# Output projection by column halves, branch products in pairs, one merge gate held, in a two-layer hybrid encoder

## The chip, the core and the metric

The program runs on one core of a Trainium2 chip. Its engines are TensorE (PE, with its weight loads PEld), VectorE (DVE), ScalarE (ACT), GpSimd (POOL) and SyncE (SP, which issues the transfers). The metric is the device time of one execution in microseconds. Before the change it is 1779.11 us, the median of three runs (1778.2 to 1780.48).

## The reference, cut to what matters

Two layers run one after the other on x (512 tokens, 1024 channels, float32):

```python
p = split(x @ w_in + b_in)
y_a, y_b, y_c = three token mixers, each times its SiLU gate      # 512 channels each
branch = einsum('nbsc,ncd->nbsd', stack([y_a, y_b, y_c]), w_branch)
gates  = sigmoid(p['merge'].reshape(B, S, 3, D))
merged = sum_n gates[n] * branch[n]
out    = merged @ w_out
x      = LayerNorm(alpha * x + out) * ln_g + ln_b
```

The third mixer is an attention of four heads over 512 tokens. Head h fills channels 128h to 128h+127 of y_c, so that the last head's channels are the last quarter of the contraction of the third branch.

## The kernel before, in words

A float32 product is made of three products of rounded parts (hi by hi, lo by hi, hi by lo). Every weight chunk of 128 x 1024 is loaded by SP, rounded on ACT (`hi`, L274) and subtracted on POOL (`lo`, L275); for the first weights of a layer the subtraction is on DVE. Chunks take turns in two raw buffers and three hi and three lo buffers. Matrix products write one of four PSUM banks `mm`. The order on each engine is set by a scheduler that simulates the program when it is built; on the chip it is fixed, and an engine waits at an instruction whose inputs are not there.

What matters here is the end of a layer. For each query tile of 128 tokens, a head of the third mixer makes scores (`msc`, five products), a softmax (DVE maximum L646, ACT exp L648, DVE reciprocal and scale L649 and L650), four transposes (`mtr`, L653), four copies by DVE and ACT in turn (L655), and the values' products (`mo`, L659). The eight merge gates of the third branch (`mg`, 24 products each, L1158) are independent of the heads and are put between these steps. After the last head, `yc3h` and `yc3l` (L663 to L666) are its gated output in hi and lo parts.

`merge_branch` (L1079) makes the branch products `br`, one bank of 128 output channels after the other; within a bank the 12 products go in the order of channel blocks (`late`, L298), so that the last head's come last. DVE multiplies by the gate, adds to `acc`, and the sum is split again (`mm`, L1161: hi on ACT, lo on DVE).

w_out is loaded as eight chunks (`wo`, L1176 to L1197): number n holds 256 input channels (n % 4) and 512 output channels (n // 4). Three chunks lie in buffers of the large pool, two in buffers of `acc`, three in the rotating weight buffers. Token tiles 0 and 1 are made first, both column halves, then their common norm (L1248), then tile 2 with its norm and tile 3 with its norm. `residual` (L1199) adds alpha*x and takes statistics on DVE; `norm` (L1204) makes the inverse root from twelve small DVE operations and applies it by two passes over 1024 columns. The last tile's first half goes over ACT (L1221) and POOL (L1222). In layer 0 the result is also transposed back for layer 1 (`xps`, L421, and the split `xl`, L425), whose first products `st` (L498) run over halves of the tokens.

Of the kernel before, what the change touches and what calls it, by code (L numbers as in the profile page):

```python
# [200 lines left out]
def tile_encoder(ctx: ExitStack, tc: tile.TileContext, x, xt, positions, blocks, wuq, wuh, par_in, brow, lbp,  # L201
# [92 lines left out]
    def mm3(ps, lhs, rhs, kt, late=False):  # L294

        steps = [(a, b, k) for a, b in PASSES for k in range(kt)]
        if late:
            steps.sort(key=lambda t: (t[2], t[1]))  # L298
        for n, (a, b, k) in enumerate(steps):
            newest["product"] = nc.tensor.matmul(ps, lhs(a, k), rhs(b, k), start=n == 0, stop=n == 3 * kt - 1)  # L300

# [157 lines left out]
    def layer(l, x_src, need_next):  # L459
# [173 lines left out]
        def mla_head(h, prep, kr, v, gate):  # L633
# [3 lines left out]
            for qt in range(NT):  # L637
# [14 lines left out]
                for kb in range(NT):  # L652
                    nc.tensor.transpose(tr[:, kb * 128:kb * 128 + 128], p[:, kb * 128:kb * 128 + 128], ident)  # L653
# [425 lines left out]
        def merge_branch(n, dp, y, gates):  # L1079
            ys = ([p[0] for p in y], [p[1] for p in y])  # L1080
            wb = w_chunk(l, ("br", n, dp), (4, 256), f"wb{n}{dp}_{l}")
            for j in range(2):
                dt_, g = 2 * dp + j, gates[j]
                ps = fm(ys, f"br{n}{dt_}_{l}", lambda a, k: wb[a][:, k, 128 * j:128 * j + 128], kt=4, late=True)
# [73 lines left out]
        gates = [merge_gate(2, dt_, held[dt_ // 4][:, dt_ % 4]) for dt_ in range(KT)]  # L1158
# [14 lines left out]
        for t, src in ((lng, ln_g), (lnb, ln_b)):  # L1173
            nc.sync.dma_start(t, bass.AP(src.tensor, src.offset + l * D, [[0, 128], [512, 2], [1, 512]]))
        wo = []
        for n in range(8):  # L1176
            name = f"wo{n}_{l}"
            if n < 3:
# [3 lines left out]
            elif n < 5:  # L1182
# [57 lines left out]
        for half in range(2):  # L1240
            banks = [mm_bank(f"wo{tt}{half}_{l}") for tt in range(2)]
            for kp in range(4):
                for tt in range(2):
                    product(banks[tt], tt, half, (kp,))
            for tt in range(2):
                for j in range(2):
                    residual(tt, 2 * half + j, banks[tt][:, 256 * j:256 * j + 256])
        norm((0, 1))  # L1248
        for tt in (2, 3):
            for half in range(2):  # L1250
                cuts = [slice(0, 256), slice(256, 512)] if tt == NT - 1 and half else [slice(0, 512)]
                for cols in cuts:
                    bank = mm_bank(f"wo{tt}{half}{cols.start}_{l}")[:, cols]
                    product(bank, tt, half, range(4), cols)
                    for j in range(cols.start // 256, cols.stop // 256):
                        residual(tt, 2 * half + j, bank[:, 256 * j - cols.start:256 * j - cols.start + 256])
# [34 lines left out]
```

## Time and profile before

| | |
|---|---|
| median of 3 runs | 1779.11 us (1778.2 to 1780.48) |
| the profiled execution | 1780.54 us, of which the trace spans 1778.8 us |
| PE busy | 1745.7 us (98%) |
| DVE, ACT, POOL busy | 1048.8, 731.7, 574.6 us |
| granted PE clock, mean | 0.995 |
| layer 0, w_out products | 839.4 to about 889.8 us, then the first products of layer 1 |
| layer 1, w_out products | 1720.3 to 1768.9 us, then DVE alone and the last transfers |

PE is busy nearly all the time, so the places where it is not, or runs at a lower clock, are read one by one. The 40-slice line of the clock shows full speed everywhere: the slices are 44 us wide, and a lower clock over a few microseconds is only seen in narrow stretches.

### The profile page before, as it was taken

The numbers are of one execution on the slowest core, as the hardware profiler recorded it, in microseconds if no ns is written. First come the engines' busy times: TensorE is split into PE (matmuls) and PEld (weight loads), VectorE is DVE, ScalarE is ACT, GpSimd is POOL, SyncE is SP. The second block draws the span as 40 slices with busy tenths as digits, with TensorE's granted clock in tenths as the row PEclk, the third lists the DMA queues.
The fourth block names the chain that finished last, engine by engine and source line by source line (L and its number), as shares of the span: only waits on it lengthen the run. The fifth ranks groups of instructions, "written<-read, shape, count | busy, mean of one in ns | idle before, by whom it ended". The sixth has DMA issues, their size and how long they took to land.

```text
span 1778.8 us, 26441 instructions
## 1 busy us (share of the span) xinstructions
PE 1745.7 (98%) x10616; PEld 1451.2 (82%) x10616; DVE 1048.8 (59%) x1886; ACT 731.7 (41%) x1273; POOL 574.6 (32%) x338
## 2 busy tenths in 40 slices
PE   9999999999999999999999999999999999999987
PEld 7778978988888888887788888888888888888876
DVE  8888777443232566656577778775333225656566
ACT  6445453242424354433254355442424244434330
POOL 0412244233333243333213122532434332333341
PEclk9999999999999999999999999999999999999999
DMA  5223222223323222422242222222323222324222
GB/s 193 83 66 102 75 73 85 79 65 95 84 72 91 62 79 74 144 81 70 95 137 89 85 78 73 88 82 74 78 66 106 72 84 46 98 74 149 76 71 71
DMA packets 77146, 154.15 MB, mean 87 GB/s; under 512 B 37728, under 2 KB 37856, under 8 KB 77024
## 3 DMA queue, kind: packets, MB, share of 16 engines
q1 hardware_dynamic: 77024, 152.47, 28.0%
q8 instruction: 83, 1.36, 0.3%
q14 instruction: 39, 0.32, 0.1%
HBM read 148.15 MB, written 4.29 MB: 86 GB/s over the span
## 4 chain that ended last, share of the span: by engine, by line
PE 61%; DVE 4%; ACT 2%; DMA 1%; issue 1%; POOL 1%; SPq 0%; DVEq 0%; ACTq 0%
PE mg L300 14%; PE dl L300 6%; PE br L300 5%; PE wo L1236 5%; PE hf L300 4%; PE dv L317 4%; PE cq L300 2%; PE hq L300 2%; PE mo L659 2%; PE ckv L300 1%; PE hgg L300 1%; PE hv L317 1%; PE do L1016 1%; PE st L498 1%; PE qn L300 1%; PE dg L300 1%
## 5 line engine op out<-in xcount | busy, mean ns | idle before, releaser
L772 DVE TENSOR_TENSOR kk<-kk,fr 128x512 f32<-128x512 f32 x96 | 93.4, 992 | 32.8 <-ACT kc L742 21.7
L693 POOL TENSOR_TENSOR qq<-hq,fr 128x1024 f32<-128x1024 f32 x16 | 42.5, 2655 | 199.3 <-DVE fr L686 179.5
L771 DVE TENSOR_TENSOR qq<-qq,fr 128x512 f32<-128x512 f32 x96 | 75.3, 797 | 17.0 <-POOL qq L693 15.2
L1076 DVE TENSOR_SCALAR mg<-mg 128x512 f32<-128x512 f32 x32 | 53.4, 1680 | 54.0 <-ACT mg L1075 53.9
L895 DVE CUSTOM_DVE_ANT_0 zb<-dsb,con 128x256 f32<-128x256 f32 x64 | 23.3, 421 | 46.4 <-PE dsb L948 46.3
L764 DVE COPY_PREDICATED ha<-mask,hs 64x256 f32<-64x256 uint8 (+1 forms) x80 | 40.4, 505 | 16.7 <-PE hs L754 15.5
L655 ACT COPY mpt<-mtr 128x128 f32<-128x128 f32 x64 | 17.1, 266 | 77.7 <-DVE mpt L655 77.7
L275 POOL TENSOR_TENSOR wb_1l<-wb_1r,wb_1h 128x1024 fp32r<-128x1024 f32 x12 | 29.4, 2449 | 58.9 <-ACT wb_1h L274 45.0
L275 POOL TENSOR_TENSOR wb_0l<-wb_0r,wb_0h 128x1024 fp32r<-128x1024 f32 x12 | 29.4, 2448 | 58.8 <-ACT wb_0h L274 44.9
L878 DVE TENSOR_SCALAR dl<-dl,par,con 128x512 f32<-128x512 f32 x24 | 25.8, 1076 | 38.0 <-PE dl L300 37.9
L754 PEld LDWEIGHTS hs<-qq,kc 128*64 128x64 f32 x1024 | 33.3, 137 | 17.6 <-issue 8.8
L732 POOL TENSOR_SCALAR_AFFINE_SELECT ha<-hc 128x256 f32<-128x256 f32 x32 | 12.8, 424 | 105.0 <-ACT hc L727 104.8
L754 PE MATMUL hs<-qq,kc 128*64 128x64 f32 x1024 | 38.2, 225 | 5.6 <-DVE qq L771 5.6
L996 ACT ACTIVATE za<-za,dst 128x256 f32<-128x256 f32 x64 | 30.0, 471 | 33.4 <-DVE dst L990 33.4
L655 DVE COPY mpt<-mtr 128x128 f32<-128x128 f32 x64 | 18.5, 289 | 39.6 <-PE mtr L653 31.6
L713 POOL TENSOR_TENSOR hk<-kk,f 128x256 f32<-128x256 f32 x32 | 23.8, 745 | 51.5 <-DVE fr L775 51.5
L789 ACT COPY hkt<-hkt 128x384 f32<-128x384 f32 x32 | 15.4, 480 | 60.3 <-PE hkt L787 59.9
L1076 DVE TENSOR_SCALAR mgc<-mgc 128x512 f32<-128x512 f32 x16 | 24.8, 1547 | 25.0 <-ACT mgc L1075 25.0
L742 ACT COPY kc<-kk 128x512 f32<-128x512 f32 x64 | 37.6, 621 | 4.2 <-DVE kk L772 4.1
L650 DVE TENSOR_SCALAR mp<-mp,mst 128x512 f32<-128x512 f32 x32 | 35.6, 1112 | 0.9
L1201 DVE SCALAR_TENSOR_TENSOR res<-res,wo 128x256 f32<-128x256 f32 x32 | 12.1, 416 | 38.1 <-PE wo L1236 38.0
L659 PE MATMUL mo<-mpt,mv 128*128 128x128 f32 (+1 forms) x192 | 33.5, 309 | 0.0
(1509 smaller groups left out, 5408.5 us busy)
## 6 DMA issues: line engine op xcount, KB each, us to landing
wb_0r<-in_blocks_dram SPq DMA_DIRECT2D x12, 512.0 KB, 3.6
wb_1r<-in_blocks_dram SPq DMA_DIRECT2D x12, 512.0 KB, 3.6
w_0r<-in_blocks_dram SPq DMA_DIRECT2D x9, 512.0 KB, 3.6
w_1r<-in_blocks_dram SPq DMA_DIRECT2D x8, 512.0 KB, 3.6
w_2r<-in_blocks_dram SPq DMA_DIRECT2D x8, 512.0 KB, 3.5
w_3r<-in_blocks_dram SPq DMA_DIRECT2D x8, 512.0 KB, 3.6
wo_0r<-in_blocks_dram SPq DMA_DIRECT2D x8, 512.0 KB, 3.5
wo_1r<-in_blocks_dram SPq DMA_DIRECT2D x8, 512.0 KB, 3.5
```

Source lines behind the costliest of these rows:

```text
L275: (eng or nc.gpsimd).tensor_tensor(lo, raw, hi.bitcast(F32), ALU.subtract)
L300: newest["product"] = nc.tensor.matmul(ps, lhs(a, k), rhs(b, k), start=n == 0, stop=n == 3 * kt - 1)
L317: nc.tensor.matmul(ps, xs[a][2 * j + k][:, toks], w[b][:, k], start=j == 0 and n == 0, stop=j == 3 and n == 5)
L659: nc.tensor.matmul(o[:, cols], v[:, kb, h * 128:h * 128 + 128], pts[kb][:, cols], start=qt == 1 and kb == 0, stop=qt == NT - 1 and kb == N ...
L693: nc.gpsimd.tensor_tensor(qq, bcast(q, [[0, 2], [1, S]]), fr, ALU.mult)
L742: made = A.copy(fap(kc, 0, [[2 * m, R // 2], [m, 2], [1, m]]), fap(kk, 0, [[2 * m, R // 2], [S + m, 2], [1, m]]))
L754: mat = nc.tensor.matmul(sc[rows, to], kc[:, at], rhs, start=True, stop=True)
L764: ready = [V.copy_predicated(fap(a[rows], cols.start, [[128, NT], [1, wd]]), bcast(mk, [[0, NT], [1, wd]]), fap(sc[rows], cols.start, [[12 ...
L771: V.tensor_tensor(fap(qq, 0, dims), fap(qq, 0, dims), qf, ALU.mult)
L772: V.tensor_tensor(fap(kk, 0, dims), fap(kk, 0, dims), kf, ALU.mult)
L1076: V.tensor_scalar(g, g, 0.5, 0.5, ALU.mult, ALU.add)
L1236: nc.tensor.matmul(ps, ms[a][2 * kp + k][:, tt * 128:tt * 128 + 128], wo[4 * half + kp][b][k][:, cols], start=(kp, a, b, k) == (0, 0, 0, 0 ...
```

## The change

1. `merge_branch` makes its two banks together: 9 products of each bank over the first three channel blocks, then 3 products of each over the last block.
2. The last of the eight merge gates of the third branch is held: its first product gets a dependence on the last head's last transpose.
3. w_out goes by column halves over all four token tiles. In the first half the four banks advance chunk by chunk; in the second half the tiles go one after the other, each followed by its own norm. The chunks' places are exchanged: 0, 4, 5 lie in the large pool, 6 and 7 in `acc`, 1 to 3 in the rotating buffers.

```diff
+            if n == 0 and "hold" in newest:
+                after(newest["product"], newest.pop("hold"))
...
-                    nc.tensor.transpose(tr[:, kb * 128:kb * 128 + 128], p[:, kb * 128:kb * 128 + 128], ident)
+                    newest["turned"] = nc.tensor.transpose(tr[:, kb * 128:kb * 128 + 128],
+                                                           p[:, kb * 128:kb * 128 + 128], ident)
...
-            for j in range(2):
+            banks = [mm_bank(f"br{n}{2 * dp + j}_{l}") for j in range(2)]
+            for ks in (range(3), range(3, 4)):
+                for j, ps in enumerate(banks):
+                    for k, a, b in [(k, a, b) for k in ks for a, b in ((0, 0), (1, 0), (0, 1))]:
+                        newest["product"] = nc.tensor.matmul(
+                            ps, wb[a][:, k, 128 * j:128 * j + 128], ys[b][k], start=(k, a, b) == (0, 0, 0),
+                            stop=(k, a, b) == (3, 0, 1))
+            for j, ps in enumerate(banks):
                 dt_, g = 2 * dp + j, gates[j]
-                ps = fm(ys, f"br{n}{dt_}_{l}", lambda a, k: wb[a][:, k, 128 * j:128 * j + 128], kt=4, late=True)
...
-        gates = [merge_gate(2, dt_, held[dt_ // 4][:, dt_ % 4]) for dt_ in range(KT)]
+        gates = []
+        for dt_ in range(KT):
+            if dt_ == KT - 1:
+                newest["hold"] = newest["turned"]
+            gates.append(merge_gate(2, dt_, held[dt_ // 4][:, dt_ % 4]))
...
-            if n < 3:
+            if n in (0, 4, 5):
...
-            elif n < 5:
+            elif n > 5:
...
-        for half in range(2):
-            banks = [mm_bank(f"wo{tt}{half}_{l}") for tt in range(2)]
-            for kp in range(4):
-                for tt in range(2):
-                    product(banks[tt], tt, half, (kp,))
-            for tt in range(2):
-                for j in range(2):
-                    residual(tt, 2 * half + j, banks[tt][:, 256 * j:256 * j + 256])
-        norm((0, 1))
-        for tt in (2, 3):
-            for half in range(2):
-                cuts = [slice(0, 256), slice(256, 512)] if tt == NT - 1 and half else [slice(0, 512)]
...
+        banks = [mm_bank(f"wo{tt}0_{l}") for tt in range(NT)]
+        for kp in range(4):
+            for tt, ps in enumerate(banks):
+                product(ps, tt, 0, (kp,))
+                if kp == 3:
+                    for j in range(2):
+                        residual(tt, j, ps[:, 256 * j:256 * j + 256])
+        for tt in range(NT):
+            for cols in [slice(0, 256), slice(256, 512)] if tt == NT - 1 else [slice(0, 512)]:
+                bank = mm_bank(f"wo{tt}1{cols.start}_{l}")[:, cols]
+                product(bank, tt, 1, range(4), cols)
+                for j in range(cols.start // 256, cols.stop // 256):
+                    residual(tt, 2 + j, bank[:, 256 * j - cols.start:256 * j - cols.start + 256])
             norm((tt,))
```

What this moves on PE at the last head of layer 0, before the change, from the last scores (`msc`, query tile 3) on:

```order
L643 MATMUL msc_0_6658<-krs_5301,rs_0_6534 128x512
L644 MATMUL msc_0_6658<-krs_5301,rs_0_6535 128x512
L300 MATMUL br_0_6961<-yc1h_6107,wb_0h 128x512
L300 MATMUL br_0_6961<-yc1h_6107,wb_0l 128x512
L300 MATMUL br_0_6961<-yc1l_6111,wb_0h 128x512
L300 MATMUL br_0_6961<-yc2h_6499,wb_0h 128x512
```

And the same place after it, where `mo` holds the values' products of query tile 2, `mtr` the last transposes and `mg` the held gate:

```order
L646 MATMUL msc_0_6658<-krs_5301,rs_0_6535 128x512
L662 MATMUL mo_0_6586<-mpt_0_6582,mv_5638 128x128
L662 MATMUL mo_0_6586<-mpt_0_6583,mv_5638 128x128
L662 MATMUL mo_0_6586<-mpt_0_6584,mv_5638 128x128
L662 MATMUL mo_0_6586<-mpt_0_6585,mv_5638 128x128
L655 MATMUL mtr_0_6670<-con,mp_0_6666 128x128 x4
L300 MATMUL mg_6928<-xh,w_13376h 128x512 x8
L300 MATMUL mg_6928<-xl,w_13376h 128x512 x8
L300 MATMUL mg_6928<-xh,w_13376l 128x512 x5
```

Before, sixteen branch products lay between the last scores and `mo` of query tile 2, six more before `mtr`, and eleven after it. Now four products stand between scores and transposes, and the gate's 21 after them.

On PE at w_out of layer 0, before, the rows behind the 24th product (tiles 0 and 1 are `wo_0_7201` and `wo_0_7202`):

```order
L1236 MATMUL wo_0_7202<-wo_0_7152,mm20h 128x512
L1236 MATMUL wo_0_7202<-wo_0_7152,mm30h 128x512
L1236 MATMUL wo_0_7201<-wo_0_7157,mmh_7115 128x512
L1236 MATMUL wo_0_7201<-wo_0_7157,mmh_7119 128x512
L1236 MATMUL wo_0_7201<-wo_0_7157,mml_7116 128x512
```

After, the rows behind the 48th product (`wo_0_7204` is tile 3):

```order
L1250 MATMUL wo_0_7204<-wo_0l,mm20h 128x512
L1250 MATMUL wo_0_7204<-wo_0l,mm30h 128x512
L1250 MATMUL wo_0_7201<-wo_0h,mmh_7115 128x512
L1250 MATMUL wo_0_7201<-wo_0h,mmh_7119 128x512
L1250 MATMUL wo_0_7201<-wo_0h,mml_7116 128x512
```

The product that first needs the third chunk and the fifth and sixth split sums (`mmh_7115`, `mmh_7119`) is now the 49th instead of the 25th.

On DVE at the very end of layer 1, before (`res_1_14580` is tile 3):

```order
L267 SCALAR_TENSOR_TENSOR lnr_1y<-lnr_1t,lnr_1y 128x1
L265 TENSOR_TENSOR lnr_1t<-lnr_1y 128x1
L266 TENSOR_TENSOR lnr_1t<-lnr_1t,lnr_1h 128x1
L267 SCALAR_TENSOR_TENSOR lnr_1y<-lnr_1t,lnr_1y 128x1
L1225 SCALAR_TENSOR_TENSOR res_1_14580<-res_1_14580,lnr_1y,lnb_14584 128x512 x2
```

And after (`res_1_14596` is tile 2, `res_1_14599` tile 3):

```order
L1239 SCALAR_TENSOR_TENSOR res_1_14596<-res_1_14596,lnr_1y,lnb_14603 128x1024
L267 SCALAR_TENSOR_TENSOR lnr_1y<-lnr_1t,lnr_1y 128x1
L265 TENSOR_TENSOR lnr_1t<-lnr_1y 128x1
L266 TENSOR_TENSOR lnr_1t<-lnr_1t,lnr_1h 128x1
L267 SCALAR_TENSOR_TENSOR lnr_1y<-lnr_1t,lnr_1y 128x1
L265 TENSOR_TENSOR lnr_1t<-lnr_1y 128x1
L266 TENSOR_TENSOR lnr_1t<-lnr_1t,lnr_1h 128x1
L267 SCALAR_TENSOR_TENSOR lnr_1y<-lnr_1t,lnr_1y 128x1
L1239 SCALAR_TENSOR_TENSOR res_1_14599<-res_1_14599,lnr_1y,lnb_14603 128x512 x2
```

Tile 2's last pass over 1024 columns now stands inside tile 3's chain of small operations. Three more DVE instructions move: the `lo` splits of layer 1's first three weights stood behind the last w_out products of layer 0 and now stand among the first half's residuals.

## Rows read from the trace of the kernel before

**Rows 1.** The page's first part: busy time, share and instructions of each engine.

```profile
PE 1745.7 (98%) x10616; PEld 1451.2 (82%) x10616; DVE 1048.8 (59%) x1886; ACT 731.7 (41%) x1273; POOL 574.6 (32%) x338
```

**Rows 2.** Waits of PE: total us, times, longest.

```profile
PE wo L1236 <- ACT wo L1191: 5.3, 2, 2.6
...
PE br L300 <- DVE yc3l L666: 2.5, 2, 1.2
...
PE br L300 <- DVE yc3h L663: 1.6, 2, 0.8
```

**Rows 3.** Stretches: length, PE, PEld, DVE, ACT, POOL busy, clock, DMA.

```profile
820.00:825.00 5.00, 4.22 (x23) 3.47 (x22) 2.22 (x4) 1.51 (x3) 0.84 (x1) 1.00 0.00 0
825.00:830.00 5.00, 3.67 (x15) 2.37 (x15) 4.41 (x5) 1.05 (x1) 2.46 (x2) 1.00 0.32 105
...
850.00:855.00 5.00, 5.00 (x17) 3.92 (x17) 1.12 (x4) 1.44 (x2) 2.75 (x4) 0.74 0.60 186
...
1730.00:1735.00 5.00, 5.00 (x17) 3.76 (x16) 0.37 (x2) 1.31 (x3) 3.46 (x3) 0.68 0.50 119
```

**Rows 4.** Timeline of PE at w_out: start, length, line, operands, [idle before].

```profile
839.45 0.39 PE L1236 MATMUL wo<-wo,mm00h 128*128 128x512 f32 x1
...
844.66 0.39 PE L1236 MATMUL wo<-wo,mm30h 128*128 128x512 f32 x1
847.69 0.73 PE L1236 MATMUL wo<-wo,mmh 128*128 128x512 f32 x2 [2.64 <-ACT wo L1191]
...
855.07 0.62 PE L1236 MATMUL wo<-wo,mm00h 128*128 128x512 f32 x2
...
1728.58 0.73 PE L1236 MATMUL wo<-wo,mmh 128*128 128x512 f32 x2 [2.65 <-ACT wo L1191]
...
1735.79 0.62 PE L1236 MATMUL wo<-wo,mm01h 128*128 128x512 f32 x2
```

**Rows 5.** Timeline of ACT before that wait.

```profile
846.07 0.62 ACT L251 CAST mmh<-acc 128x512 fp32r<-128x512 f32 x1 [1.06 <-DVE acc L1090]
846.60 1.04 ACT L1191 CAST wo<-wo_0r 128x1024 fp32r<-128x1024 f32 x1
```

**Rows 6.** Timeline of PE at the last head of layer 0.

```profile
801.97 1.30 PE L300 MATMUL mg<-xh,w_13376h 128*128 128x512 f32 x5
...
808.35 1.89 PE L659 MATMUL mo<-mpt,mv 128*128 128x256 f32 x8
809.89 1.04 PE L300 MATMUL mg<-xh,w_13376l 128*128 128x512 f32 x3
```

**Rows 7.** Timeline of DVE at the last head.

```profile
792.23 0.41 DVE L1076 TENSOR_SCALAR mgc<-mgc 128x512 f32<-128x512 f32 x1
...
802.89 2.05 DVE L1076 TENSOR_SCALAR mgc<-mgc 128x512 f32<-128x512 f32 x1 [2.80 <-ACT mgc L1075]
...
814.60 0.68 DVE L646 TENSOR_REDUCE mst<-msc 128x1 f32<-128x512 f32 x1
...
816.39 0.48 DVE L650 TENSOR_SCALAR mp<-mp,mst 128x512 f32<-128x512 f32 x1
```

**Rows 8.** Timeline of ACT and POOL at the last head.

```profile
800.40 1.05 ACT L274 CAST wb_0h<-wb_0r 128x1024 fp32r<-128x1024 f32 x1 [2.32 <-issue]
...
802.27 2.39 POOL L275 TENSOR_TENSOR wb_0l<-wb_0r,wb_0h 128x1024 fp32r<-128x1024 f32 x1 [3.05 <-ACT wb_0h L274]
```

**Rows 9.** Timeline between the layers: DVE splits, then PE's wait.

```profile
889.67 1.22 DVE L275 TENSOR_TENSOR w_0l<-w_0r,w_0h 128x1024 fp32r<-128x1024 f32 x1
...
901.46 1.33 PE L421 MATMUL xps<-con,res 128*128 128x128 f32 x8 [1.76 <-issue]
```

**Rows 10.** Timeline of DVE at the end of layer 1.

```profile
1767.63 1.28 DVE L1225 SCALAR_TENSOR_TENSOR res<-res,lnr_1y,lnb 128x1024 f32<-128x1024 f32 x1
1768.94 0.42 DVE L1201 SCALAR_TENSOR_TENSOR res<-res,wo 128x256 f32<-128x256 f32 x1
...
1774.16 1.41 DVE L1225 SCALAR_TENSOR_TENSOR res<-res,lnr_1y,lnb 128x512 f32<-128x512 f32 x2
```

More of the change, by code (lines that the diff above doesn't have):

```diff
@@ L1237, in product @@
                                  start=(kp, a, b, k) == (0, 0, 0, 0), stop=(kp, a, b, k) == (3, 0, 1, 1))
-        for half in range(2):
-            banks = [mm_bank(f"wo{tt}{half}_{l}") for tt in range(2)]
-            for kp in range(4):
-                for tt in range(2):
-                    product(banks[tt], tt, half, (kp,))
-            for tt in range(2):
-                for j in range(2):
-                    residual(tt, 2 * half + j, banks[tt][:, 256 * j:256 * j + 256])
-        norm((0, 1))
-        for tt in (2, 3):
-            for half in range(2):
-                cuts = [slice(0, 256), slice(256, 512)] if tt == NT - 1 and half else [slice(0, 512)]
[L1252 to L1256, printed above, removed]
+        banks = [mm_bank(f"wo{tt}0_{l}") for tt in range(NT)]
[11 more added lines that the diff above has]
+                    residual(tt, 2 + j, bank[:, 256 * j - cols.start:256 * j - cols.start + 256])
             norm((tt,))
```

## The prediction

> **What bounds the kernel now.** The page's first part shows PE busy for 98% of the span [rows 1]. The reader is to see there that no other engine can be the bound over the whole, and that only about 33 us of PE's time are left to win by closing gaps. So the second view is PE's waits: the largest group is w_out waiting for ACT, 5.3 us in two waits, and then the branch products waiting for DVE's `yc3l` and `yc3h`, 2.5 and 1.6 us in two waits each [rows 2]. Each is one wait per layer. The third view is narrow stretches with the granted clock: behind the w_out wait the clock is 0.74 and 0.68 over 5 us, while around the two branch waits of layer 0 it stays at 1.00 [rows 3]. The fourth is PE's timeline at w_out: the 24th product starts at 844.66, the 25th at 847.69 after 2.64 us of idling [rows 4]. From 839.45 to 844.66 there are 23 steps, 0.227 us each. The 24 products from 847.69 to 855.07 take 7.38 us instead of 24 x 0.227 = 5.44, so the lower clock (1.2 instead of 2.4 GHz for a part of them) costs another 1.94 us. In layer 1 it is 2.65 us of idling and 7.21 - 5.44 = 1.77 us [rows 4].
>
> **w_out by halves.** ACT shows what the wait was: the third w_out chunk's rounding (846.60, 1.04 us) stands behind the last split sum (846.07) in ACT's order [rows 5], and that one waits for DVE's last `acc`. The 25th product needs that chunk. Now the product that needs the third chunk and the fifth and sixth sums is the 49th, 48 x 0.227 = 10.9 us after the start instead of 5.4, and the one that needs the seventh and eighth is the 73rd, at 16.3 us. The third chunk was there 847.64 - 839.45 = 8.2 us after the start of w_out, so even with ACT's and DVE's old pace the new place is 2.7 us late enough; besides, ACT's order now has chunks two to four ahead of the last sums. The second half needs four more chunks from 21.8 us on, each with an ACT rounding of 1.05 us and a POOL subtraction of 2.4 us, beside transfers that are then two chunks ahead; I cost them at nothing. If the cover is gone (DVE more than 2.7 us late), the old wait returns in part. The term is -(2.64 + 1.94) - (2.65 + 1.77) = **-9.0 us**. Its bounds are 0 and -9.0; I take the far end, because the margin is larger than any DVE delay that the rows show.
>
> **Pairs and the held gate.** The number of products is the same. What goes are the two waits of 0.78 and 1.25 us per layer (1.6 + 2.5 = 4.1 us in all [rows 2]): the gate's last 3 products and 20 branch products now lie between `mo` and the first use of `yc3h`, 23 x 0.227 = 5.2 us, against three DVE operations over 512 columns, put at the 0.68 us of the maximum [rows 7], and up to 2.4 us more if POOL holds one up [rows 8]. What comes is a place without filler before it. In the order of the change only four products stand between the last scores and the last transposes, and those need the softmax. From the start of the maximum (814.60) to the end of the scale (816.39 + 0.48) it takes 2.27 us [rows 7].
>
> I walk it with zero at the end of the gate before the held one. In the old trace this point is 801.97 [rows 6], and POOL's subtraction of the next branch chunk starts 0.30 us after it (802.27, 2.39 us [rows 8]). The ACT rounding of a branch chunk (1.05 us [rows 8]) must wait for the 16th product of that gate and stands ahead of the exp of query tile 2, so this exp ends near 0.24 and the scale would start at 0.47, behind POOL. DVE's gate operation of the same kind takes 0.41 us at 792.23, where POOL is idle, and 2.05 us at 802.89, where POOL runs since 802.27; it ends 0.28 us after POOL [rows 7, 8]. So the scale ends at 0.30 + 2.39 + 0.28 = 2.97. PE reaches the transposes of query tile 2 after `mo`, 809.89 - 808.35 = 1.54 us [rows 6], and starts them at 3.05: 1.5 us idle. Then four transposes of a quarter of a product's columns (about 0.2 us at the pace of 0.227), five scores (1.1) and four `mo` with half the columns of the earlier four (0.8) keep PE until 5.2. The last score started at 4.2 and takes 0.39, the length of a product [rows 4]; from 4.6, 2.27 us of softmax and a hop of 0.1 give 7.0 for the last transposes: 1.8 us idle. Together 3.3 us per layer. If the scale comes 0.2 us earlier than POOL, the first wait goes, but the copies then stand behind the gate operation in POOL's shadow, and I get about 1.2 + 1.1 = 2.3 us. If both scales are held up, it is 3.3 + 2.05 = 5.3 us. A lower bound is zero, if the chip runs the softmax ahead of this walk. I take 3.3, the case of the row at 802.89. Net of the 2.03 us that go, the term is 2 x 1.27 = **+2.5 us**, between -4.1 and +6.5.
>
> **Between the layers.** PE now waits 1.76 us for the transposes of the last tile [rows 9]. DVE did three splits of layer 1's first weights (1.22 us each [rows 9]) in front of that tile's norm; they move under the first half, where DVE has little to do. But four norms now fall into the second half, and I find small new waits for tile 1's norm and split at the end of w_out, 0.2 + 0.5 us. Net **-1.0 us**, between -1.8 (no new wait) and +2 (three splits' worth of backlog kept back).
>
> **The end of layer 1.** Before, the last residual starts at 1768.94 and the last pass at 1774.16: 5.2 us [rows 10]. Now tile 2's last pass over 1024 columns, 1.28 us of which 1.19 count [rows 10], stands inside tile 3's chain, with two or three small operations: **+1.4 us**. The bounds are +1.0 and, with tile 2's 512 KB transfer then still under way beside the last two, +2.1.
>
> **Sum.** -9.0 + 2.5 - 1.0 + 1.4 = -6.1 us. The profiled execution took 1780.54 us (its span of 1778.8 and 1.7 around it), which gives 1774.4. That execution is 1.4 us over the median of the runs, 1779.11; for the median the forecast is **1773.0 us**.
>
> **Rivals.**
>
> *The clock falls at the last head.* The 2.65 us gap brought the clock down; two new gaps of 1.5 and 1.8 us within 6 us, with transposes and short products between, could as well, for 1.8 us per layer: 1773.0 + 3.7 = 1776.7. Against it: the old gaps of 0.78 and 1.25 us, 3.4 us apart, left the clock at 1.00 [rows 3], and each new gap is shorter than the one that did it. For it: less work lies between the new ones. The Trainium skill speaks for this rival (TensorE: Matmul & The Clock Gate, "A second HAM failure mode: psum-queue depth-cycling"): there frequent short idling between groups of products makes the clock oscillate. The two stretches at 1.00 show that two gaps alone do not always do it; by that rule the time would be this rival's, by the rows the forecast's.
>
> *The w_out wait only moves.* If DVE, with pairs of bank readings coming together and POOL's subtractions holding up its additions, is over 2.7 us later than now, the 49th product waits instead of the 25th. Then the term of -9.0 falls away and the others remain: 1779.1 + 2.9 = 1782.0. For it speaks that DVE's operations were stretched to 2.05 us at such places [rows 7]; against it, the 5.4 us that the product was moved.
>
> *The norms pile up: slower.* All four norms now lie in the second half. From the last residual to the last pass tile 3 takes 5.2 us, and a pass over 1024 columns 1.28 us [rows 10]: 6.5 us of DVE per tile, if nothing is interleaved, and PE brings a tile every 24 x 0.227 = 5.45 us. Then the last tile is 4 x 6.5 - 21.8 = 4.2 us late in layer 1, and in layer 0, with two splits of the transposed tile (2 x 0.68, as the maximum [rows 7]), 4 x 7.9 - 21.8 = 9.8 us late. The time is 1779.1 - 9.0 + 2.5 + 4.2 + 1.4 + 9.8 = 1788.0. It makes the kernel slower from about 9 us of backlog in both layers together. Against it: the order puts the small operations of one tile between the larger ones of the next, where they cost little, and the layer-0 splits of weights have gone from there.
>
> **How the numbers follow.** Forecast 0.70, clock at the last head 0.14, the w_out wait 0.08, the norms 0.08. The forecast's terms that are least sure are the last head and the passage between the layers, some 3 us to either side, which gives 1769 to 1776.5. Taking in the clock rival, the range is 1768.0 to 1779.0; above it lie the other two, 0.16, and a little is left below. A difference of 0.2% (3.6 us) is about what a measurement of this kernel can tell from none, so faster means under 1775.6 and slower over 1782.7. Of the forecast about 0.64 lies under 1775.6, and of the clock rival 0.05, where it strikes one layer only: faster 0.69. The rest of these two and most of the w_out rival make 0.22 for the same; slower has 0.09.
>
> **What would show it.** In the changed profile, PE's waits should have no w_out wait for ACT over 0.5 us, and the clock should be at 1.00 in the 10 us behind the start of w_out: the -9.0 term. Two waits for DVE's `mp` per layer, before the transposes of query tiles 2 and 3, of 1 to 2 us each, should stand there, and none for `yc3h` or `yc3l`. A clock under 1.00 in these stretches is the first rival. The wait for `xps` should be under 1 us, and from the last product to the last pass it should be 6.5 us instead of 5.2. The forecast is wrong if w_out still waits, or if PE idles over 5 us at the last head.

## The result, and the profile after

The changed kernel took 1771.7 us (median of 6 runs, 1769.9 to 1772.2), the kernel before beside it 1780.4 us: a ratio of 0.9945, with a 95% interval from 0.9934 to 0.9956. The forecast was 1773.0. The profiled execution took 1771.63 us with a span of 1769.9, which is 8.9 us less than that of before; the working below compares these two.

Page of the changed kernel, first part, which answers to [rows 1]:

```profile
PE 1741.8 (98%) x10616; PEld 1450.5 (82%) x10616; DVE 1064.2 (60%) x1912; ACT 730.3 (41%) x1273; POOL 573.8 (32%) x338
```

PE is still the bound. Its waits, which answer to [rows 2] (total us, times, longest):

```profile
PE mtr L655 <- DVE mp L652: 5.2, 4, 1.5
...
PE xps L423 <- DVE res L1239: 0.8, 1, 0.8
PE wo L1250 <- DVE res L1215: 0.6, 1, 0.6
```

The w_out wait for ACT and both waits of the branch products are gone. In their place stand two waits per layer for the softmax (`mp`), 1.09 and 1.48 us, and one small wait at w_out of layer 0.

Stretches behind the start of w_out, which answer to [rows 3] (clock in the third last column):

```profile
850.00:855.00 5.00, 5.00 (x23) 4.14 (x23) 0.00 (x0) 1.35 (x3) 4.71 (x3) 1.00 0.42 138
...
1730.00:1735.00 5.00, 5.00 (x23) 4.13 (x22) 2.04 (x7) 1.14 (x2) 3.20 (x3) 1.00 0.24 95
```

23 products in 5 us at clock 1.00, where there were 17 at 0.74 and 0.68.

The timeline of PE in layer 0, from the last head to layer 1's first transposes, which answers to [rows 4, 6, 9]:

```profile
803.34 1.89 PE L662 MATMUL mo<-mpt,mv 128*128 128x256 f32 x8
806.32 0.66 PE L655 MATMUL mtr<-con,mp 128*128 128x128 f32 x4 [1.09 <-DVE mp L652]
...
810.53 0.66 PE L655 MATMUL mtr<-con,mp 128*128 128x128 f32 x4 [1.48 <-DVE mp L652]
...
839.18 0.39 PE L1250 MATMUL wo<-wo,mm00h 128*128 128x512 f32 x1
...
861.65 0.47 PE L1250 MATMUL wo<-wo,mm00h 128*128 128x512 f32 x1 [0.55 <-DVE res L1215]
...
885.67 1.09 PE L423 MATMUL xps<-con,res 128*128 128x128 f32 x8 [0.80 <-DVE res L1239]
```

And what holds up the first of these transposes, on DVE and on POOL:

```profile
803.72 2.55 DVE L652 TENSOR_SCALAR mp<-mp,mst 128x512 f32<-128x512 f32 x1
```
```profile
803.64 2.34 POOL L275 TENSOR_TENSOR wb_0l<-wb_0r,wb_0h 128x1024 fp32r<-128x1024 f32 x1 [4.67 <-PE mg L300]
```

The scale of query tile 2 starts 0.08 us behind POOL's subtraction and takes 2.55 us, where the one of [rows 7] took 0.48. It ends 0.29 us after POOL does.

Timeline of DVE at the end of layer 1, which answers to [rows 10]:

```profile
1759.10 0.42 DVE L1215 SCALAR_TENSOR_TENSOR res<-res,wo 128x256 f32<-128x256 f32 x1 [0.15 <-PE wo L1250]
...
1761.55 1.18 DVE L265 TENSOR_TENSOR lnr_1t<-lnr_1y 128x1 f32<-128x1 f32 x1
...
1762.84 1.28 DVE L1239 SCALAR_TENSOR_TENSOR res<-res,lnr_1y,lnb 128x1024 f32<-128x1024 f32 x1
...
1765.47 1.42 DVE L1239 SCALAR_TENSOR_TENSOR res<-res,lnr_1y,lnb 128x512 f32<-128x512 f32 x2
```

From the last residual to the last pass it is 6.4 us instead of 5.2: tile 2's pass over 1024 columns stands inside tile 3's chain.

### The profile page after: what moved, and what is told of

Its sections match the earlier page's. It is cut to its first block, busy times and chain, and to the rows that moved or that the text cites. A ratio compares the mean times of both kernels' runs of the same rounds, so it can differ in the third digit from the quotient of the medians.

```text
span 1769.9 us, 26458 instructions
## 1 busy us (share of the span) xinstructions
PE 1741.8 (98%) x10616; PEld 1450.5 (82%) x10616; DVE 1064.2 (60%) x1912; ACT 730.3 (41%) x1273; POOL 573.8 (32%) x338
## 3 DMA queue, kind: packets, MB, share of 16 engines
q8 instruction: 83, 1.36, 0.3%
## 5 line engine op out<-in xcount | busy, mean ns | idle before, releaser
L1099 DVE TENSOR_TENSOR acc<-acc,mgc 128x512 f32<-128x512 f32 x16 | 32.2, 2049 | 0.0
L1004 ACT ACTIVATE zb<-zb,dst 128x256 f32<-128x256 f32 x64 | 31.6, 495 | 0.0
```

## The experiments

Twelve kernels ran in three groups of four; each group ran on a chip of its own, with the kernel before beside it. On the chips of the first two groups the kernel before took 1790.9 and 1790.8 us (scattered over 8 and 6 us), on that of the third 1780.2. The whole times are therefore given as ratios to the kernel before of the same group. The stretches that the change touches are read from the traces, where the changed kernel's repeat to within 0.1 us on another chip: from layer 0's first gate of the last branch (`w_12480h`) to the first w_out product ("last head" below), w_out itself, from there to layer 1's first HGRN product ("passage"), and from the last product to the last pass ("tail").

**w_out by halves alone.** The loop over the columns and the chunks' places, with branch products and gates as before.

> Part 3 alone: the kernel before with w_out by halves of its columns over all four token tiles (loop, and places of its chunks), its branch products and merge gates as before. Theory A (the parts add up, each worth what the two traces show): two w_out waits with their lower clock -9.0, the passage between the layers -0.6, the end of layer 1 +1.1, so -8.5 us against the kernel before, 1772 on a base of 1780.4. No w_out wait for ACT over 0.5 us, clock 1.00 behind the start of w_out; the branch products still wait 0.8 and 1.25 us per layer for yc3h and yc3l. Theory B (the last head did cost the +2.5 us that was forecast, and w_out is worth more than was counted): -11.4 us, 1769. Theory C (the pairs let the last sums come in time, and without them the w_out wait only moves to the 49th product): -2 to -5 us, with a wait for ACT or DVE left at w_out.

Measured: 0.9982 [0.9973, 0.9991], -3.1 us. The time is the one that theory C gave, and a wait for DVE is left at w_out, but not at the 49th product and not for the last sums, so none of the three has the mechanism. The wait for ACT is gone, but w_out takes 47.9 and 45.2 us instead of 45.7 and 44.0 in the changed kernel. PE's waits of this kernel:

```profile
PE br L300 <- DVE yc3l L666: 2.5, 2, 1.3
PE wo L1236 <- DVE mgc L1089: 1.8, 2, 0.9
PE br L300 <- DVE yc3h L663: 1.6, 2, 0.8
PE wo L1236 <- DVE res L1201: 1.5, 1, 1.5
```

The wait for `mgc` stands at the seventh product (the later expectations put it at the 19th): it takes the second bank, which DVE's gate multiplication of a branch product still has to read. DVE's four additions ahead of it and POOL's work beside them, in this kernel:

```profile
832.05 5.96 DVE L1090 TENSOR_TENSOR acc<-acc,mgc 128x512 f32<-128x512 f32 x4
```
```profile
831.05 2.40 POOL L275 TENSOR_TENSOR wb_0l<-wb_0r,wb_0h 128x1024 fp32r<-128x1024 f32 x1 [2.53 <-ACT wb_0h L274]
833.41 2.85 POOL L275 TENSOR_TENSOR wo_0l<-wo_0r,wo_0h 128x1024 fp32r<-128x1024 f32 x1
```

And in the kernel before:

```profile
830.08 3.77 DVE L1090 TENSOR_TENSOR acc<-acc,mgc 128x512 f32<-128x512 f32 x4
```
```profile
829.08 2.41 POOL L275 TENSOR_TENSOR wb_0l<-wb_0r,wb_0h 128x1024 fp32r<-128x1024 f32 x1 [2.54 <-ACT wb_0h L274]
835.01 2.89 POOL L1192 TENSOR_TENSOR wo<-wo_0r,wo 128x1024 fp32r<-128x1024 f32 x1 [3.52 <-ACT wo L1191]
```

A w_out chunk is split earlier here: POOL's second subtraction follows the first at once, DVE's additions take 5.96 us instead of 3.77, and what comes behind them is late for w_out. The gate multiplication that frees the second bank starts at 843.15, 1.7 us behind the first w_out product; in the kernel before the same one, at 838.98, stood 0.5 us ahead of it. Whether the chunks' places or the new order of the products brought the subtraction forward, this run does not part. The stretches add up to about -5 us against the first trace of the kernel before; the 2 us between this and the measured -3.1 stay open.

**Pairs and held gate alone.** w_out as before.

> Parts 1 and 2 alone: branch products in pairs and the held gate, w_out as before. Theory A: the 2.03 us of waits for yc3h and yc3l per layer give way to 2.57 us before the transposes of query tiles 2 and 3, and the restart after each old wait cost some more than its idle time, so -0.5 to +0.5 us, about 1780. Theory B (the forecast's term): +2.5 us, 1783. Theory C (the pairs help at every branch, not only at the last head): -2 us or more. w_out keeps its wait of 2.6 us per layer with the lower clock behind it; if the sums come earlier by the pairs, that wait is shorter.

Measured: 0.9980 [0.9971, 0.9989], -3.9 us. The trace shows theory A at the last head (85.59 us, as in the changed kernel). w_out is 0.6 and 1.5 us shorter than in the kernel before (its wait is 4.2 us in two instead of 5.3), the passage 1.3 us longer; that makes under 1 us. The other 3 us lie outside these stretches. By the size of the total this would be theory C, but the first two traces, which have pairs in one and not in the other, speak against it: from the start to the last branch's first gate the changed kernel takes 1.36 us more than the kernel before in layer 0, and from the first HGRN product to that gate 1.76 us more in layer 1, of which 1.59 us each are products that moved there (below). So the pairs gain nothing at the other branches on that chip. Without a trace of the kernel before from this chip the 3 us stay open.

**The changed kernel without the held gate.** The line that sets `newest["hold"]` is left out.

> The changed kernel without the held gate: pairs and w_out by halves stay. In this order 36 branch products lie between and behind the last transposes as filler, the mo products of query tile 3 come after 21 of them, and the first product that needs yc3h comes right behind mo. Theory A (the hold trades one stall for another): no wait before the transposes of query tiles 2 and 3, but yc3h and yc3l are waited for, 0.8 and up to 1.3 us per layer, as in the kernel before: within 1 us of the changed kernel, -8 to -9.5 against before. Theory B (the hold is worth what it was built for): the two waits are longer than 2.6 us per layer and the time is 2 us or more above the changed kernel. Theory C (the hold does harm): 2 us or more below it, -11 against before.

Measured: 0.9975 [0.9965, 0.9985], -5.7 us, against -11.0 for the changed kernel itself on a chip with the same base (below). The last head takes 85.60 us, so on that stretch theory A is right: the hold trades one stall for another of the same price. But w_out is 50.0 and 45.3 us. DVE's first multiplication of a branch product shows why, here first without and then with the held gate:

```profile
830.03 2.48 DVE L1098 TENSOR_TENSOR mgc<-mgc,br 128x512 f32<-128x512 f32 x4 [0.59 <-PE br L1089]
```
```profile
823.74 1.28 DVE L1098 TENSOR_TENSOR mgc<-mgc,br 128x512 f32<-128x512 f32 x2 [2.61 <-PE br L1089]
```

w_out starts at 841.80 in the one and at 839.18 in the other. Without the hold DVE begins 11.8 us ahead of it, with the hold 15.4. These 3.6 us are what spares the wait for `mgc`; so the parts are not independent. All twelve kernels with w_out by halves (the first trace among them) go by this lead: the four that have 11.8 us wait for `mgc`, and the eight that have 14.3 us or more do not. The two waits of w_out that this kernel has, and its clock:

```profile
PE wo L1250 <- DVE res L1215: 2.0, 1, 2.0
PE wo L1250 <- DVE mgc L1098: 1.9, 2, 1.0
```
```profile
865.00:870.00 5.00, 3.05 (x8) 2.50 (x8) 4.69 (x10) 1.04 (x1) 0.00 (x0) 0.70 0.70 210
```

**Two gates held, each a query tile earlier.**

```diff
-                    newest["turned"] = nc.tensor.transpose(tr[:, kb * 128:kb * 128 + 128],
+                    newest["turned", qt] = nc.tensor.transpose(tr[:, kb * 128:kb * 128 + 128],
...
+        HOLD = {6: 1, 7: 2}
         for dt_ in range(KT):
-            if dt_ == KT - 1:
-                newest["hold"] = newest["turned"]
+            if dt_ in HOLD:
+                newest["hold"] = newest["turned", HOLD[dt_]]
```

> The changed kernel with two merge gates held, each one query tile earlier: the seventh gate's products only after the last head's transposes of query tile 1, the eighth's only after those of query tile 2. So 22 gate products stand before the transposes of query tile 2, 18 before those of query tile 3, and 36 branch products of two pairs before the first use of yc3h. Theory A (the two new waits for mp are missing filler, and 2.27 us of softmax fit under 18 products, 4.1 us): both waits go, no new one comes, 2 x 2.57 us = -5.1 us against the changed kernel, -14 against before, 1766.5. The scale of query tile 2 may still be held behind POOL (2.5 us instead of 0.49), and that costs nothing then. Theory B (a wait shifts rather than goes: the transposes of query tile 1 now have 16 products before them instead of 30, or yc3h is late): 1 to 2.5 us of new waits per layer, so -5 to 0 against the changed kernel. Theory C (the chip's softmax at the last head is so slow by POOL's hold that 18 products do not hide it): a wait of 0.5 to 1 us before the transposes of query tile 2 or 3 stays, -3 to -4.

Measured: 0.9944 [0.9931, 0.9957], -11.9 us. At the last head it is theory A: no wait for `mp`, none for `yc3h`, and 83.00 us in each layer instead of 85.58. But DVE begins its branch products 11.8 us ahead of w_out again, and the wait for `mgc` is back:

```profile
PE wo L1251 <- DVE res L1216: 2.0, 1, 2.0
PE wo L1251 <- DVE mgc L1098: 1.7, 2, 0.9
```

**The changed kernel again,** as base of the second group.

> The changed kernel once more, unaltered, as the base for the three kernels run beside it and as a test of what the change is worth apart from the chip that it was first timed on: the first four experiments ran beside a kernel before of 1790.9 us instead of 1780.4, and there w_out by halves alone gave only -3 us and parts 1 and 2 alone -4. Theory A (the parts help each other: with the gate held, DVE has caught up at the start of w_out, and the wait of 0.9 us for DVE's mgc at the 19th product, seen in each of the three kernels with w_out by halves there, isn't in it): -8 to -10 us against before, no wait for mgc, a wait for res of 0.5 to 2 us. Theory B (that chip has slower transfers, and the change is worth less on such a chip whatever its parts): -5 to -7 us, with the wait for mgc.

Measured: 0.9940 [0.9928, 0.9952], -11.0 us, no wait for `mgc`, 0.6 us for `res`: theory A. Its stretches are those of the first trace: last head 85.59, w_out 45.75 and 43.99, passage 21.2 (21.26 there), tail 6.40.

**Four gates held.** As with two, `{4: 0, 5: 1, 6: 2, 7: 3}`.

> The changed kernel with four merge gates held instead of one: the fifth to the eighth gate's products each only after the last head's transposes of query tiles 0, 1, 2 and 3. So 24, 22 and 18 gate products stand before the transposes of query tiles 1, 2 and 3, and the eighth gate still covers yc3h and yc3l as in the changed kernel. Theory A (the two waits for mp are missing filler, and nothing else moves): both go, -5.1 us against the changed kernel, -14 against the kernel before, and no wait for mgc at w_out. Theory B (the two-gate kernel had the wait for mgc, 0.9 us per layer, because its branch products ran out of yc-free rows and came late, all at once; here they come as in the changed kernel, but the held gates' own tanh and scale now come late): -3 to -4 against the changed kernel, with a wait for mgc of 0.9 us per layer. Theory C (the softmax is held up by POOL so long that 18 products do not hide it): a rest of 0.5 to 1 us per layer before one of the transposes.

Measured: 0.9986 [0.9976, 0.9996], 8 us above the changed kernel: all theories were wrong. The last heads take 89.56 and 88.44 us. The waits before query tiles 2 and 3 went, but one of 4.0 us came before those of query tile 0, and the clock fell to half behind it:

```profile
789.82 1.12 PE L655 MATMUL mtr<-con,mp 128*128 128x128 f32 x4 [3.99 <-DVE mp L652]
```
```profile
790.00:795.00 5.00, 5.00 (x14) 4.05 (x15) 1.53 (x5) 1.31 (x4) 0.00 (x0) 0.50 0.21 80
```

DVE was late there all along; 32 gate products, now held back, had covered it:

```profile
786.98 2.05 DVE L526 SCALAR_TENSOR_TENSOR mg3s<-mg3s,mg3z 128x512 f32<-128x512 f32 x1
788.96 0.41 DVE L1079 TENSOR_SCALAR mgc<-mgc 128x512 f32<-128x512 f32 x1
789.29 0.47 DVE L652 TENSOR_SCALAR mp<-mp,mst 128x512 f32<-128x512 f32 x1
```

In the changed kernel of this group that scale is as late (789.38), but PE gets to the transposes only at 792.96. Filler, products that PE can do while it would otherwise wait, has to be taken from where it covers nothing.

**The residuals ahead of the first weight split.** One order on DVE: `w_0l` of layer 1 only behind the first half's last residual.

> The changed kernel with one order more on DVE: the first lo split of layer 1's first weights (w_0l) only behind the residuals of the first half of layer 0's w_out. The 97th product waited 0.55 us for DVE's residual of tile 0, which stood behind that split, and that one waited for its weights' transfer. Theory A (the split blocks the residual): the wait for res at w_out of layer 0 goes, -0.55 us against the changed kernel where transfers are quick, up to -2 where they are slow as in the first four experiments; the split itself is not missed before the first product of layer 1. Theory B (the residual comes late by itself, after its own product and tile load): the wait stays. Against before -8.5 to -11.

Measured: 0.9928 [0.9915, 0.9941], 0.9 us below the changed kernel, which the totals alone would not part; the trace does. The wait for `res` is gone and w_out of layer 0 is 44.86 us instead of 45.75: theory A. The split had blocked the residual while it waited for its own weights.

**Four gates, residuals first, short inverse square root.**

```diff
-            V.tensor_tensor(t, y, y, ALU.mult)
-            V.tensor_tensor(t, t, h, ALU.mult)
+            if n == 1:
+                V.scalar_tensor_tensor(t, y, y, h, ALU.mult, ALU.mult)
+            else:
+                V.tensor_tensor(t, y, y, ALU.mult)
+                V.tensor_tensor(t, t, h, ALU.mult)
```

The short form is used where the root is for one tile (`n == 1`).

> Four gates held, the residuals ahead of the split, and a shorter inverse square root where it is for one tile: each of its three steps makes y*y*h in one scalar_tensor_tensor instead of two tensor_tensor operations (9 small operations become 6; the chip's chain shows 0.19 us from one to the next). Theory A (each hides nothing of the others): -5.1 for the gates, -0.5 to -2 for the residuals, and -0.6 to -1.6 at the end of layer 1, where the last pass starts 6.4 us after the last product (one of the small operations takes 1.18 us there beside POOL's multiplication instead of 0.16): 6 to 8.5 us below the changed kernel, -15 to -17 against the kernel before. Theory B (the small operations lie under the larger passes and the transfers at the end): the last pass still starts 6.2 us or more after the last product, and the gain is that of the gates and the residuals alone, -5.5 to -7.

Measured: 0.9962 [0.9948, 0.9977]; the four gates spoil it as above. The short form gives 0.42 us at the end (tail 5.98) and 0.7 us in the passage (20.5): less than theory A said at the end, more than B.

**POOL's subtraction behind the scale.** In the changed kernel the subtraction of the last branch's first weight chunk waits for the scale of query tile 2.

> The changed kernel with one order more: POOL's subtraction of the first branch weight chunk of the last branch waits until DVE's scale of query tile 2 of the last head is done. Theory A (the scale took 2.55 us instead of 0.49 because POOL's subtraction had started 0.1 us before it): the scale takes 0.5 us again, the transposes of query tile 2 come right behind mo, the wait of 1.09 us goes, the one before query tile 3 stays at 1.3 to 1.7 us: 1.0 to 1.5 us less from the first gate to w_out in each layer (85.6 to 84.3), -2 to -3 us against the changed kernel. Theory B (the scale is late by its own chain, exp behind ACT's rounding, and POOL only runs at the same time): the wait of 1.09 us stays, and the time is that of the changed kernel.

Measured: 0.9941 [0.9928, 0.9955] (four executions, so the total tells little); last head 84.64 and 84.61 us, 0.95 less in each layer. The first wait is gone, the second is 1.85 us:

```profile
805.08 0.60 PE L657 MATMUL mtr<-con,mp 128*128 128x128 f32 x4
```
```profile
803.73 0.49 DVE L654 TENSOR_SCALAR mp<-mp,mst 128x512 f32<-128x512 f32 x1
...
808.67 0.85 DVE L654 TENSOR_SCALAR mp<-mp,mst 128x512 f32<-128x512 f32 x1
```
```profile
804.44 4.80 POOL L275 TENSOR_TENSOR wb_0l<-wb_0r,wb_0h 128x1024 fp32r<-128x1024 f32 x2 [12.53 <-ACT mgc L1080]
```

The first chunk's subtraction stood at 796.58 in the changed kernel; the one that held the scale (803.64) is the second's, which follows it on POOL, and both now run from 804.44. The scale takes 0.49 us at the same place and moment (803.73, where it was 2.55 at 803.72), with nothing changed but POOL. So POOL held it, theory A. The next wait then took back a third of the gain: the second subtraction now ends at 809.24 and stretches the scale of query tile 3 to 0.85 us, where it took 0.49.

**Chunks in their old places.** `n < 3` and `n < 5` as before, the loop of the changed kernel.

> The changed kernel with the w_out chunks in their old places (0 to 2 in the large buffers, 3 and 4 in those of the branch sums, 5 to 7 in the rounding buffers); the order of the products is that of the changed kernel. Theory A (the order of the products alone takes the wait away; where the chunks lie does not matter): no wait over 0.5 us for ACT or POOL at the 49th or 73rd product, w_out 44 to 46 us, time as the changed kernel within 1 us. Theory B (the fourth chunk now has to wait until the last branch sums have been read, as its buffers are theirs, and is rounded too late for the 73rd product, 16.3 us after the start): a new wait of 1 to 4 us per layer at that product, with a lower clock behind it where it is over 2.5 us, 2 to 9 us above the changed kernel.

Measured: 0.9954 [0.9940, 0.9967], no wait of w_out over 0.2 us, w_out 44.9 and 44.1 us: theory A. The order of the products took the wait away, not the places. In layer 0 w_out is even 0.8 us shorter than in the changed kernel, but the passage takes 22.56 us instead of 21.26: the new places gain there, and nothing at w_out.

**Split gate, residuals first, short inverse square root.** The seventh gate behind the transposes of query tile 1; the eighth's first 12 products behind those of query tile 2, the others behind those of query tile 3; the branch products behind the last `mo`.

```diff
             if n == 0 and "hold" in newest:
                 after(newest["product"], newest.pop("hold"))
+            if n == 12 and "mid" in newest:
+                after(newest["product"], newest.pop("mid"))
```

> The changed kernel with the seventh gate held to the last head's transposes of query tile 1, the first half of the eighth gate's products to those of query tile 2 and its second half to those of query tile 3; the branch products only behind the head's last mo products; the residuals ahead of the first weight split; and the short inverse square root. Theory A: 22 and 14 products before the transposes of query tiles 2 and 3 are enough (3.2 us and four mo, against 2.27 us of softmax), 12 gate and 24 branch products cover yc3h, and the first pair's products end early enough that DVE has caught up at w_out (no wait for mgc, which cost the two-gate kernel 0.9 us per layer): last head 83.0 us from the first gate to w_out instead of 85.6, w_out 44.9 and 44.0 us, tail 6.0: 2 x 2.6 + 0.9 + 0.4 + 0.7 = 7.2 us below the changed kernel, -18 against a kernel before of 1790.8 (or 1764.5 on a base of 1780.4). Theory B (DVE is late as soon as the gate doesn't cover the whole of yc3h's chain): mgc waits of 0.9 us per layer, -5.4 against the changed kernel.

> The two-gate kernel with the residuals ahead of the first weight split and the short inverse square root. Theory A (the three add up): last head 83.0 us, a wait for mgc of 0.9 us in each layer's w_out, no wait for res, tail 6.0: against the kernel before -11.9 (the two-gate kernel) - 2.0 (its wait for res) - 1.1 = -15. Theory B (the wait for res was the same DVE lateness as the wait for mgc and stays): -13.

Measured: 0.9904 [0.9889, 0.9919] for the split gate (1763.5 us), 0.9923 [0.9910, 0.9935] for the two gates (1767.3 us). In the split-gate kernel the last head takes 82.64 us, w_out 44.88 and 43.99, the passage 20.48 and the tail 5.97, and neither `mp`, `yc3h`, `mgc` nor `res` is waited for. This is theory A, and the fastest kernel of the study: its interval lies below that of the changed kernel. The two-gate kernel keeps its waits for `mgc` and has none for `res`, as its theory A had it, but its -12.9 us are the time that theory B gave (-13, against -15). POOL still stretches the tail, as DVE and POOL of the split-gate kernel show:

```profile
1753.60 2.17 DVE L1253 SCALAR_TENSOR_TENSOR res<-res,lnr_1y,lnb 128x1024 f32<-128x1024 f32 x1
```
```profile
1753.42 1.27 POOL L1250 TENSOR_TENSOR res<-res,lng 128x512 f32<-128x512 f32 x1 [26.66 <-ACT res L1249]
```

## Why the prediction came close, and where it was off

That the forecast of 1773.0 lies only 1.3 us from the measured 1771.7 is in part luck. It put the change at -6.1 us from a base of 1779.1; measured side by side the change is -8.7 us from 1780.4. The base came out 1.3 us higher, and that took half of the error away.

Of the 8.9 us between the two profiled executions, by the terms of the sum:

| term | forecast | measured |
|---|---|---|
| w_out, both layers | -9.0 | -4.78 - 4.59 = -9.4 |
| between the layers | -1.0 | 21.26 - 21.58 = -0.3 |
| last heads | +2.5 | -0.1 |
| end of layer 1 | +1.4 | 6.40 - 5.25 = +1.15 |
| elsewhere | 0 | -0.3 (the rest) |
| sum | -6.1 | -8.9 |

**w_out** came as worked out: the idling and the low clock behind it both went, in both layers. The reason given (the 49th product instead of the 25th) was right: the wait for ACT is also gone without the pairs and the held gate (first experiment), and without the new places (the old chunk places). The new order with none of the rest was not run. The cover named for it, DVE no more than 2.7 us late, was the weak point: w_out alone lost 2.2 and 1.2 us to DVE's `mgc` and `res`, and it was the held gate that spared the changed kernel this. I had not seen that POOL's chunk subtractions, now earlier, would stretch DVE's additions under the last branch products. The rival of a moved w_out wait has its real form there, though not at the product that it named.

**Between the layers** the wait for `xps` fell from 1.76 to 0.80 us; the small waits of 0.2 and 0.5 us that I found in the walk were 0.24 (for `xh`) and 0.55 (for `res`, which lies inside w_out). Yet the whole stretch is only 0.3 us shorter; the 0.4 us that are missing between the two I have not traced.

**The last heads** are the step that failed, by size. "Net of the 2.03 us that go, the term is 2 x 1.27": the walk itself was close. With zero at 803.34 the transposes of query tile 2 start at 2.98 (walked: 3.05) and those of tile 3 at 7.19 (7.0), and POOL's shadow, shown by the kernel with the later subtraction, is the cause that was named. But new gaps were priced from step to step, and the old ones by the idle time in the trace. An idle entry begins where the last product's modelled end lies, and says nothing of what follows the stop. In the kernel before, at the wait of 1.25 us:

```profile
825.50 0.39 PE L300 MATMUL br<-yc3h,wb_0l 128*128 128x512 f32 x1
827.14 1.20 PE L300 MATMUL br<-yc3l,wb_0h 128*128 128x512 f32 x4 [1.25 <-DVE yc3l L666]
828.42 0.50 PE L300 MATMUL br<-yc0h,wb_0h 128*128 128x512 f32 x1
```

From 825.50 to 828.42 there are five steps, 5 x 0.227 = 1.14 us without a wait; it took 2.92, so the stop cost 1.78: the idle entry, 0.16 between the next product's usual start and the last one's modelled end, 0.11 at the first step behind the stop, and 0.25 before the product at 828.42. Like with like, against the two-gate kernel, whose stretch of 83.00 us holds no wait: the changed kernel's waits cost 85.58 - 83.00 = 2.58 us per layer. The kernel before needs 87.21 us, but its stretch holds four transposes and five scores more (the gate starts one query tile earlier in its order; 1.59 us in the changed kernel's rows), so its waits cost 87.21 - 1.59 - 83.00 = 2.62. The kernel without the held gate shows the same with no subtraction: it has the changed kernel's products in this stretch and the old waits (0.79 and 1.25 us), and takes 85.60. The change at the last head was worth nothing; I had old waits at 2.03 and new ones at 3.3. How much of the error lies in either depends on the base: the split-gate kernel does the same products in 82.64 us, and from there both kinds of wait cost 0.36 more, 2.98 and 2.94. Of the new ones, the first was walked too long: PE is ready for the transposes of query tile 2 at 1.73 us from zero where nothing holds them (805.08 - 803.35 in the kernel with the later subtraction), not 1.54.

**The end of layer 1** was +1.15 of +1.4, by the mechanism named.

**The rivals.** The clock stayed at 1.00 at the last head, between and behind gaps of 1.09 and 1.48 us (layer 0 of the changed kernel, clock in the third last column; layer 1 shows 1.00 as well):

```profile
805.00:810.00 5.00, 2.95 (x19) 2.30 (x17) 3.05 (x7) 1.31 (x4) 0.98 (x1) 1.00 0.31 105
810.00:815.00 5.00, 4.47 (x22) 3.77 (x23) 1.05 (x3) 0.59 (x3) 0.00 (x0) 1.00 0.02 3
```

So the first rival is refuted for these gaps. The oscillation that the Trainium skill describes (TensorE: Matmul & The Clock Gate, "A second HAM failure mode: psum-queue depth-cycling"), which was set beside it, did not come from two gaps per layer in this kernel. The norms did not pile up: the last pass is 1.15 us later relative to the last product, and layer 1 starts 0.3 us earlier relative to the end of w_out.

**A reading that was wrong.** The prediction calls w_out's wait for ACT the largest group of PE's waits. In the view of [rows 2] one line stands above it, which is not shown there:

```profile
PE hs L754 <- DVE qq L771: 5.6, 7, 1.0
```

These seven waits lie in the first mixer (HGRN), and no term of the sum rests on their rank.

## What to carry to other kernels

Price a wait from the start of the last product before it to the start of a product well behind it, never by the idle column, and price old and new waits in the same way. Where an edit brings work of one engine forward, look at what that engine holds up there: an engine with slack on average can be the late one at that moment, and an edit next door may be what gives it time. Before filler work is moved into a gap, look at what it covers where it stands now.

## What the runs showed of the hardware

- Some DVE operations that start behind a POOL subtraction or multiplication last until POOL is done, and up to 1.1 us longer: 2.55 us instead of 0.49 for a scale over 512 columns, 2.17 instead of 1.28 for a pass over 1024, and 1.18 instead of 0.16 for a square over one column. Others do not: in the changed kernel POOL subtracts from 784.08 to 786.64, and there a reciprocal at 784.98 takes 0.15 us, while a multiplication of two SBUF tiles at 785.09 takes 2.11, which with POOL idle took 0.69 (788.70 in the kernel before). The Trainium skill (SBUF — State Buffer, "Who interferes with whom") says that the two engines share a pair of ports, that a DVE instruction with two SBUF inputs contends with a GpSimd instruction that reads SBUF, and that in DVE's two-port modes, which a `tensor_scalar` can enter, whoever issues first has the pair for the whole instruction; the rows agree, and the kernel in which only POOL's work was moved shows the hold of the scale apart from everything else.
- The clock behind a stop was not settled by the length of the stop alone. Behind 1.95 us it was 0.50 from 867 to 870 us in the kernel without the held gate (its row above, 0.70, takes in the stop), which is the lower of the two levels; behind 1.96 us at the same product of the two-gate kernel the row stays at 1.00:

```profile
865.00:870.00 5.00, 5.00 (x22) 4.17 (x23) 4.37 (x12) 2.10 (x2) 0.00 (x0) 1.00 0.45 153
```

  Behind 3.99 us PE ran its next products at half speed (the row at 0.50 above). What decides between the two cases of 1.95 us the runs don't show.
- The same kernel differed from group to group: the kernel before took 1780 us in two groups of runs and 1791 in two others. In the latter PE shows waits at the dilated attention (`do` for ACT's `dta31p`, 2.1 to 4.0 us in all) that are 1.3 us or less in the former. Each group had a chip and a time of its own, and the runs do not tell which of the two matters. What the change is worth came out alike on both kinds (0.9945 and 0.9940).
